# Softmax attention: moving three small PSUM users from the banks of P and V to the banks of the scores

## The chip, the core and the metric

The kernel runs on one NeuronCore of a Trainium2 chip. TensorE (PE in the profile; PEld is its weight load) multiplies and writes only to PSUM, VectorE (DVE) and ScalarE (ACT) read PSUM and work on it, GpSimd (POOL) works beside them, and SyncE (SP) issues most DMAs. Every engine takes its instructions in the order in which they were queued. The metric is the device time of one execution in microseconds (us); lower is better.

## The reference

The model is a trunk of two layers over 16 learned meta tokens and 1024 frames of width 1024 (T = 1040 positions). Each layer normalises, makes one wide projection, feeds it to two groups of attention heads, projects the concatenated result back and adds it, and then runs a gated feed-forward network. The change lies in the second head group, the softmax attention with a forget gate:

```python
logits = (jnp.einsum('bqhd,bkhd->bhqk', q_b, kf)
          + c_b[..., None] - c_k[:, :, None, :])
logits = jnp.where(key_pos[None, :] <= q_pos[:, None], logits, -jnp.inf)
return jnp.einsum('bhqk,bkhd->bqhd', jax.nn.softmax(logits, axis=-1), vf)
...
o_fox = rms_norm(o_fox, fox_norm[i].reshape(FOX_HEADS, FOX_DH))
```

There are 8 heads of width 64. The output of every head is normalised by its own root mean square and scaled before the output projection.

## The kernel before

Activations are kept transposed, with the 1024 features on 8 x 128 partitions and positions along the free axis. A float32 product is made of three float32r products of a high and a low part (`mm3`, lines 217 to 219: high by high, low by high, high by low), so most PE time stands on these lines. A layer runs through a gated linear attention (the `gla_` functions), the softmax attention (the `fox_` functions), the output projection, and the feed-forward network (`ffn_up`, `down_tiles`, `down_last`).

**The softmax stage.** `fox` (line 756) goes through 4 pairs of heads. The 1040 positions are cut into 9 query tiles, the first of 112 rows and the others of 116, which are taken in groups (7,8), (5,6), (3,4), (1,2), (0). A step is one query tile of one head: 72 steps per layer. In step `n`:

- `fox_scores` (line 638) makes the scores against all keys up to the tile's end, in up to three pieces: keys 0 to 459, 460 to 923 and 924 to 1039. Tiles 0 to 3 have one piece, tiles 4 to 7 two, tile 8 three, the third of them 116 keys short. Each piece takes one PSUM bank of the tag `S`: two matmuls (653, 654), then DVE adds the gate and keeps a running minimum of the negated scores (656), then, after the last piece's minimum, ACT takes the exponential with its row sum (668) and writes P to SBUF. With that the bank is free.
- `fox_transposes` (line 675) turns each piece of P by PE transposes into a PSUM bank of the tag `tr` (689; 682 for the short third piece, `ci == 2`), and ACT and DVE split it into a high and a low part in SBUF (331, 332). After DVE the bank is free.
- `fox_av` (line 692) multiplies P by V into a bank of the tag `av` (707), over all pieces of a group, and ACT copies the sum out (710). V carries its high and low part side by side, so that the sum's two halves must be added later.
- `fox_fold` (line 712) turns that result back by PE transposes (720) into a bank, the tile `fo`, where ACT (723) and DVE (724) add the two halves; then come the norm's small instructions.
- `fox_store` (line 739) transposes the normalised output again (746) into a bank, the tile `tr`, and ACT writes it with its scale (753) to SBUF for a DMA on POOL's queue (754). For the last pair it is split straight into the operand of the output projection (334, 335).

**What sets the order.** `fox_schedule` (line 827) sets delays: the transposes of step `n` are traced in step `n+2`, the products with V in `n+3` after the last tile of a group, fold in `n+4`, store in `n+6`. Between them, `work.run` traces matmuls of other work as filling: the projections of the next pair of heads (`fox_products`), a gate of the linear attention (`gr_products`), and at the end the output projection. `high_priority(8)` puts the scores a little ahead. This trace order is a priority only. Before the run, a planner with durations of its own decides the order on every engine: it takes the first instruction, by priority, whose inputs and whose buffer are free by its own clock. A tile's tag names the buffers it may take. On the chip this order is fixed, and semaphores hold an instruction whose input or buffer isn't free yet, and with it all that is queued behind it on its engine.

**The eight PSUM banks** of the stage are handed out in `attention` (line 866): two for `mm` (the filling's sums), three for `S`, two for `tr`, one for `av`. The transposes of V (587, in `fox_products`) take `tr` as well.

Of the kernel before, what the change touches and what calls it, by code (L numbers as in the profile page):

```python
# [10 lines left out]
F32 = mybir.dt.float32  # L11
# [122 lines left out]
class Kern:  # L134
# [540 lines left out]
    def fox_transposes(self, i, ci, P, PT, qoff, pp):  # L675
        nc = self.nc
        rows = self.rows_of(i)
        id_ = self.ident[:rows, :rows]
        tr = pp.tile([128, 4, 128], F32, tag="tr", name="tr")
        qs = slice(qoff, qoff + rows)  # L680
        if ci == 2:
            nc.tensor.transpose(tr[:FT, 0, :FT], P[:FT, :FT], id_)
            self.split(PT[2][:, 0, :], PT[2][:, 1, :], tr[:FT, 0, :FT])
            return
        nt = min(4 * ci + 4, i + 1) - 4 * ci
        for j in range(nt):
            t = 4 * ci + j
            o, w = self.start_of(t) - self.start_of(4 * ci), FT if i else FIRST
            nc.tensor.transpose(tr[:w, j, :rows], P[:rows, o:o + w], id_)  # L689
        self.split(PT[ci][:w, :nt, 0, qs], PT[ci][:w, :nt, 1, qs], tr[:w, :nt, :rows])  # L690
# [21 lines left out]
    def fox_fold(self, tiles, avs, den, ap, pp):  # L712
        nc = self.nc
        nt = len(tiles)
        rows = self.rows_of(tiles[0])
        fo = pp.tile([128, 2, 2, 2, 64], F32, tag="av", name="fo")
        for ti in range(nt):
            for e in range(2):
                w = rows
                nc.tensor.transpose(fo[:w, ti, e].rearrange("p a b -> p (a b)"),  # L720
                                    avs[:, e, FT * ti:FT * ti + w], self.ident[:])
        f = ap.tile([128, 2, 2, 64], F32, tag="ff", name="ff", bufs=1)
        nc.scalar.copy(f[:rows, :nt], fo[:rows, :nt, :, 0])
        nc.vector.tensor_tensor(out=f[:rows, :nt], in0=fo[:rows, :nt, :, 1], in1=f[:rows, :nt], op=ALU.add)
        on = sq = ap.tile([128, 2, 2, 64], F32, tag="fon", name="fon", bufs=1)
        nc.scalar.activation(sq[:rows, :nt], f[:rows, :nt], AF.Square)
        vv, d2, y0, a = (ap.tile([128, 2, 2], F32, tag=f"f{x}", name=f"f{x}", bufs=2)[:rows, :nt] for x in "vdya")
        nc.vector.scalar_tensor_tensor(out=d2, in0=den[:rows, :nt], scalar=64.0 * EPS,
                                       in1=den[:rows, :nt], op0=ALU.mult, op1=ALU.mult)
        nc.vector.tensor_reduce(out=vv, in_=sq[:rows, :nt], axis=AX.X, op=ALU.add)  # L730
        nc.vector.tensor_tensor(out=vv, in0=vv, in1=d2, op=ALU.add)
        fl = (lambda x: x) if nt == 2 else (lambda x: x[:, 0, :])
        self.rsqrt(fl(y0), fl(vv), fl(y0), fl(a), scale=1.0 / 64)
        for ti in range(nt):
            nc.vector.tensor_tensor(out=on[:rows, ti], in0=f[:rows, ti],
                                    in1=y0[:, ti, :].unsqueeze(2).to_broadcast([rows, 2, 64]), op=ALU.mult)
        return on

    def fox_store(self, lyr, p, tiles, on, ap, pp, mix):
        nc = self.nc  # L740
        n = FT * (len(tiles) - 1) + self.rows_of(tiles[-1])
        tr = pp.tile([128, 4, 128], F32, tag="tr", name="tr")
        trf = tr[:].rearrange("p a b -> p (a b)")
        for ti in range(len(tiles)):
            w = self.rows_of(tiles[ti])
            nc.tensor.transpose(trf[:, FT * ti:FT * ti + w],
                                on[:w, ti].rearrange("p a b -> p (a b)"), self.ident[:w, :w])
        c0 = self.start_of(tiles[0])
        if mix is not None:
            self.split(mix[0][:, c0:c0 + n], mix[1][:, c0:c0 + n], trf[:, :n], self.v(lyr, V_XN, p))  # L750
            return
        st = ap.tile([128, 2 * FT], F32, tag="fst", name="fst", bufs=1)
        nc.scalar.mul(st[:, :n], trf[:, :n], self.v(lyr, V_XN, p))
        nc.gpsimd.dma_start(self.mixd[4 + p][:, c0:c0 + n], st[:, :n])
# [689 lines left out]
```

## Time and profile before

| | |
|---|---|
| median of 3 runs | 2629.63 us (2625.71 to 2631.41) |
| the profiled execution's own time | 2631.03 us |
| its span, first to last instruction | 2629.3 us |
| mean granted TensorE clock | 0.989 |
| PE / PEld busy | 2526.3 us (96%) / 2407.3 us (92%) |
| DVE / ACT / POOL busy | 1751.8 us (67%) / 1241.9 us (47%) / 402.9 us (15%) |
| softmax stage of layer 0 / layer 1 | about 176 to 525 us / about 1480 to 1850 us |

How to read it: a row of waits tells which instruction an engine stood at and which instruction of another engine released it. For a tile's bank that means the reader who was last to leave the bank's earlier content. "PE tr L689 <- DVE PT L332" is a transpose that waited until DVE had finished with the bank. The views by time give the busy time of each engine in a stretch, and PEclk, the granted share of TensorE's full clock in it.

### The profile page before, as it was taken

To read this page: it belongs to the slowest core of one execution; us is meant where nothing else is said; L and a number is where in the kernel's file an instruction comes from. 1 tells how busy PE (TensorE), PEld (TensorE's weight loads), DVE (VectorE), ACT (ScalarE), POOL (GpSimd) and SP (SyncE) were. 2 spreads that over 40 slices of the span, in tenths; PEclk is the share of its full clock that TensorE was granted. 3 is DMA by queue.
4 is the path that set the end of the run, shared out by engine and by line. 5 is a ranking of instruction groups with operands and counts; after the bars stand their busy time and mean duration, and the time that the engine had idled before them with its cause. 6 is when DMAs were issued, how large, how long until landed. Compare 5 with 4: busy or idle time off the path is not lost.

```text
span 2629.3 us, 46309 instructions
## 1 busy us (share of the span) xinstructions
PE 2526.3 (96%) x18102; PEld 2407.3 (92%) x18102; DVE 1751.8 (67%) x3514; ACT 1241.9 (47%) x2677; POOL 402.9 (15%) x566
## 2 busy tenths in 40 slices
PE   8999999899999999999999999998999999999997
PEld 7988898898999999999999888888899999998886
DVE  7655766759877777643665665666698677776335
ACT  6345665635544445321443565665464444453112
POOL 4033333310000000000201333332100000000002
PEclk9999999999999999999999999999999999999999
DMA  3222123342322223522311222142523222245222
GB/s 124 67 83 71 44 86 122 105 145 89 105 77 83 80 81 100 209 90 59 106 52 66 75 73 74 56 133 92 164 73 113 79 79 74 84 154 179 62 57 75
DMA packets 117355, 245.96 MB, mean 94 GB/s; under 512 B 14752, under 2 KB 36512, under 8 KB 117136
## 3 DMA queue, kind: packets, MB, share of 16 engines
q1 hardware_dynamic: 97440, 184.89, 22.4%
q0 software_dynamic: 17824, 55.80, 6.2%
q8 instruction: 142, 2.33, 0.3%
q10 hardware_dynamic: 1872, 2.31, 0.2%
q14 instruction: 77, 0.63, 0.1%
HBM read 179.26 MB, written 50.91 MB: 88 GB/s over the span
## 4 chain that ended last, share of the span: by engine, by line
PE 76%; DVE 12%; issue 4%; ACT 4%; DMA 2%; POOL 1%; SPq 0%; DVEq 0%; POOLq 0%; ACTq 0%
PE mm L217 12%; PE mm L218 12%; PE mm L219 12%; PE up L217 9%; PE up L219 9%; PE up L218 9%; PE av L707 2%; PE tr L689 2%; DVE S L656 2%; PE wo L217 1%; PE wo L218 1%; PE wo L219 1%; DVE PT L332 1%; DVE x L1044 1%; DMA cb<-cd 1%
## 5 line engine op out<-in xcount | busy, mean ns | idle before, releaser
L217 PE MATMUL up<-x,hi 128*128 128x260 f32 (+1 forms) x2464 | 698.9, 284 | 2.3 <-ACT x L1043 1.6
L219 PE MATMUL up<-x,hi 128*128 128x260 f32 (+1 forms) x2464 | 697.8, 283 | 1.9 <-DVE x L1044 1.8
L218 PE MATMUL up<-x,lo 128*128 128x260 f32 (+1 forms) x2464 | 697.5, 283 | 0.8 <-DVE lo L1020 0.8
L219 PEld LDWEIGHTS up<-x,hi 128*128 128x128 f32 x2464 | 466.5, 189 | 2.9 <-DVE x L1044 2.9
L217 PEld LDWEIGHTS up<-x,hi 128*128 128x128 f32 x2464 | 465.9, 189 | 3.5 <-ACT x L1043 2.2
L218 PEld LDWEIGHTS up<-x,lo 128*128 128x128 f32 x2464 | 466.3, 189 | 1.0 <-DVE lo L1020 1.0
L217 PE MATMUL mm<-xh,hi 128*128 128x348 f32 (+4 forms) x1056 | 365.2, 346 | 0.0
L218 PE MATMUL mm<-xh,lo 128*128 128x348 f32 (+4 forms) x1056 | 340.9, 323 | 0.0
L219 PE MATMUL mm<-xl,hi 128*128 128x348 f32 (+4 forms) x1056 | 340.7, 323 | 0.0
L1020 DVE TENSOR_TENSOR lo<-raw,hi 128x512 fp32r<-128x512 f32 x308 | 210.1, 686 | 140.2 <-ACT hi L1019 140.2
L184 ACT CAST hi<-raw 128x512 fp32r<-128x512 f32 (+1 forms) x264 | 143.1, 544 | 334.0 <-PE mm L219 238.1
L218 PE MATMUL mm<-ah,lo 128*128 128x400 f32 (+1 forms) x760 | 266.5, 351 | 0.9 <-DVE lo L186 0.9
L219 PE MATMUL mm<-al,hi 128*128 128x400 f32 (+1 forms) x760 | 265.4, 349 | 0.0
L217 PE MATMUL mm<-ah,hi 128*128 128x400 f32 (+1 forms) x760 | 265.4, 349 | 0.0
L1019 ACT CAST hi<-raw 128x512 fp32r<-128x512 f32 x308 | 190.3, 621 | 113.8 <-PE up L219 87.2
L186 DVE TENSOR_TENSOR lo<-raw,hi 128x512 fp32r<-128x512 f32 (+1 forms) x196 | 110.8, 569 | 175.3 <-ACT hi L184 171.6
L217 PEld LDWEIGHTS mm<-xh,hi 128*128 128x128 f32 x1056 | 201.0, 190 | 6.0 <-issue 5.3
L218 PEld LDWEIGHTS mm<-xh,lo 128*128 128x128 f32 x1056 | 200.9, 190 | 0.4 <-issue 0.3
L219 PEld LDWEIGHTS mm<-xl,hi 128*128 128x128 f32 x1056 | 199.8, 189 | 0.4 <-issue 0.3
L668 ACT ACTIVATE P<-S,m 116x460 f32<-116x460 f32 (+2 forms) x224 | 125.1, 562 | 76.2 <-DVE m L656 72.1
L332 DVE TENSOR_TENSOR PT<-tr,PT 116x464 fp32r<-116x464 f32 (+3 forms) x240 | 122.1, 516 | 57.5 <-ACT PT L331 55.9
L218 PEld LDWEIGHTS mm<-ah,lo 128*128 128x128 f32 x760 | 142.8, 188 | 14.6 <-DVE lo L186 1.5
(248 smaller groups left out, 5106.5 us busy)
## 6 DMA issues: line engine op xcount, KB each, us to landing
raw<-in_wm_dram SPq DMA_DIRECT2D x338, 256.0 KB, 2.7
raw<-in_wd_dram SPq DMA_DIRECT2D x64, 256.0 KB, 2.7
actd<-cv POOLq DMA_DIRECT2D x22, 520.0 KB, 3.0
st<-actd SPq DMA_DIRECT2D x22, 520.0 KB, 4.6
actd<-cv POOLq DMA_DIRECT2D x22, 512.0 KB, 2.9
st<-actd SPq DMA_DIRECT2D x22, 512.0 KB, 4.9
cb<-cd SPq DMA_DIRECT2D x16, 520.0 KB, 4.2
kA<-kA SPq DMA_DIRECT2D x24, 260.0 KB, 3.8
```

The costliest lines, as they stand in the source:

```text
L184: nc.scalar.copy(hi[:, :n, :], raw[:, :n, :])
L186: eng.tensor_tensor(out=lo[:, :n, :], in0=raw[:, :n, :], in1=hi[:, :n, :].bitcast(F32), op=ALU.subtract)
L217: nc.tensor.matmul(ps, wh, xh[:, c0:c0 + n], start=first, stop=False, skip_group_check=more)
L218: nc.tensor.matmul(ps, wl, xh[:, c0:c0 + n], start=False, stop=False, skip_group_check=more)
L219: nc.tensor.matmul(ps, wh, xl[:, c0:c0 + n], start=False, stop=last, skip_group_check=more)
L332: nc.vector.tensor_tensor(out=lo, in0=src, in1=hi.bitcast(F32), op=ALU.subtract)
L656: nc.vector.tensor_tensor_reduce(out=S[:rows, :n], in0=S[:rows, :n], in1=cb[:rows, c0:k1], scale=1.0, scalar=(BIG if ci == 0 else m[:rows, ...
L668: nc.scalar.activation(P[:rows, :n], S[:rows, :n], AF.Exp, scale=-1.0, bias=m[:rows, nch - 1:nch], accum_out=(den if nch == 1 else d3[:row ...
L689: nc.tensor.transpose(tr[:w, j, :rows], P[:rows, o:o + w], id_)
L707: nc.tensor.matmul(av[:, a:width], w.rearrange("p a b -> p (a b)"), x, start=(t == 0 and i == 0), stop=(t == last and i == 1))
L1019: nc.scalar.copy(hi[:], src[:])
L1020: nc.vector.tensor_tensor(out=lo[:], in0=src[:], in1=hi[:].bitcast(F32), op=ALU.subtract)
```

## The change

Three tiles take a bank of another tag; nothing else is touched. The short third piece's transpose (8 per layer) and the output's transpose in `fox_store` (20 per layer) leave the two `tr` banks for the three `S` banks. The folded sums `fo` (20 per layer) leave the one `av` bank for the `S` banks. The numbers of banks per tag stay as they are.

```diff
@@ fox_transposes
-        tr = pp.tile([128, 4, 128], F32, tag="tr", name="tr")
+        tr = pp.tile([128, 4, 128], F32, tag="S" if ci == 2 else "tr", name="tr")
@@ fox_fold
-        fo = pp.tile([128, 2, 2, 2, 64], F32, tag="av", name="fo")
+        fo = pp.tile([128, 2, 2, 2, 64], F32, tag="S", name="fo")
@@ fox_store
-        tr = pp.tile([128, 4, 128], F32, tag="tr", name="tr")
+        tr = pp.tile([128, 4, 128], F32, tag="S", name="tr")
```

## The prediction

> **What bounds the kernel now.** I read the page first, then the busy times of the two softmax stages, then who waited for whom.
>
> ```profile
> span 2629.3 us, 46309 instructions
> PE 2526.3 (96%) x18102; PEld 2407.3 (92%) x18102; DVE 1751.8 (67%) x3514; ACT 1241.9 (47%) x2677; POOL 402.9 (15%) x566
> PE 76%; DVE 12%; issue 4%; ACT 4%; DMA 2%; POOL 1%; SPq 0%; DVEq 0%; POOLq 0%; ACTq 0%
> ```
>
> TensorE sets the time: 96% busy, and 76% of the chain that ended last. So the change is worth what it takes out of, or puts into, PE's idle time. The busy time by stretch (columns: stretch, its us, then busy us and instructions of PE, PEld, DVE, ACT, POOL, then PEclk, DMA share, GB/s):
>
> ```profile
> 176.00:525.00 349.00, 322.50 (x2221) 302.87 (x2219) 234.88 (x730) 212.85 (x636) 120.89 (x174) 0.99 0.28 85
> 1480.00:1850.00 370.00, 340.28 (x2316) 320.30 (x2315) 241.85 (x749) 216.98 (x649) 123.46 (x176) 0.98 0.28 84
> 476.00:496.00 20.00, 15.80 (x106) 14.28 (x105) 20.00 (x55) 16.67 (x47) 9.30 (x14) 0.91 0.46 145
> 1780.00:1800.00 20.00, 15.38 (x96) 13.71 (x95) 20.00 (x55) 15.60 (x45) 10.17 (x16) 0.83 0.51 159
> ```
>
> In the softmax stages PE is idle for 349 - 322.5 = 26.5 us and 370 - 340.3 = 29.7 us: 56 us that a better use of banks could touch. DVE is busy two thirds of the stage, but in one stretch of each layer, at the last pair of heads, all of it; waits there are DVE's own pace and no bank cures them. Who PE waited for (total us, times, longest):
>
> ```profile
> PE tr L689 <- DVE PT L332: 23.1, 22, 2.0
> PE tr L682 <- DVE PT L332: 12.1, 6, 3.4
> PE av L707 <- DVE ff L724: 8.8, 15, 1.0
> PE tr L746 <- DVE PT L332: 3.6, 8, 1.3
> PE tr L689 <- DVE ml L335: 1.0, 1, 1.0
> PE mm L218 <- POOL lo L186: 4.1, 6, 1.0
> PEld S L653 <- ACT P L668: 1.1, 4, 0.4
> ```
>
> The first five rows are all waits for a bank of `tr` or of `av`: 48.6 us of the 56. The scores, with three banks, waited 1.1 us in four places. That imbalance is what the change uses.
>
> **The work itself doesn't change.** All 16 short transposes, 144 fold transposes and 72 output transposes remain, with their readers on ACT and DVE and the store's DMA on POOL's queue; a bank of another tag makes none of them longer. What moves is who waits for which bank, and the planner's order with it.
>
> **Removed 1: the short piece, L682.** Here is one of its six waits, PE's rows first, then DVE's.
>
> ```profile
> 370.01 0.33 PE L707 MATMUL av<-PT,Vm 116*128 116x116 f32 x2
> 372.33 0.31 PE L682 MATMUL tr<-ident,Ps 116*116 116x116 f32 x1 [1.98 <-DVE PT L332]
> 372.40 0.40 PE L217 MATMUL mm<-xh,hi 128*128 128x344 f32 x1
> ...
> 368.67 0.34 DVE L616 TENSOR_SCALAR ge<-gx 128x348 f32<-128x348 f32 x1 [0.34 <-DMA mixd<-ge]
> 371.20 0.52 DVE L621 SCALAR_TENSOR_TENSOR ge<-ge,gy 128x348 f32<-128x348 f32 x1 [1.21 <-ACT gy L619]
> 371.63 0.63 DVE L332 TENSOR_TENSOR PT<-tr,PT 116x464 fp32r<-116x464 f32 x1
> ```
>
> The first two pieces hold both `tr` banks while ACT and DVE are late with them, behind a gate (L616 to L621) that waited for its DMA. The short piece, third in line, stands at the head of PE's queue, and filling that needs nothing (L217) stands behind it. With a bank of `S` it goes on as soon as one of three is free. I take 10 of the 12.1 us; what isn't got is where ACT, late as well, holds the scores' banks. Ends: 6 and 12.1.
>
> **Removed 2: the clock after these waits.** The granted clock behind three of the six:
>
> ```profile
> 373.10:376.60 3.50, 3.50 (x16) 3.32 (x15) 2.33 (x8) 0.79 (x2) 0.99 (x2) 0.51 0.31 102
> 1584.80:1588.30 3.50, 3.47 (x13) 3.30 (x14) 2.40 (x7) 0.76 (x3) 0.56 (x1) 0.51 0.32 102
> 1673.60:1680.50 6.90, 5.53 (x21) 5.35 (x22) 4.67 (x12) 3.49 (x11) 0.99 (x2) 0.51 0.16 52
> ```
>
> PE works at half clock for 3.5, 3.5 and 6.9 us right after. At 0.51, its 3.50 + 3.47 + 5.53 us of work there would take half: 6.1 us lost. Not every such gap does it, so other gaps may start to; I take 4 us, ends -6 (as much lost elsewhere) and 6.1. The Trainium skill, page "TensorE: Matmul & The Clock Gate", section "Why this matters for your kernels", warns only of idle gaps over about 3 us. The trace speaks against that: the gap of 1.98 us was enough. By the page's rule the longest wait alone (the 3.4) would count, the clock term would be 5.53 x 0.49 = 2.7 us, and the sum 1.3 us later.
>
> **Removed 3: `fo` in the bank of P and V, and the store in `tr`.** One wait of each, DVE's row that released the first above it, then the store and the transpose behind it, that one's last case, and the first and last of two transposes behind a short piece:
>
> ```profile
> 213.97 0.42 DVE L724 TENSOR_TENSOR ff<-fo,ff 116x256 f32<-116x256 f32 x1
> 214.44 1.16 PE L707 MATMUL av<-PT,V 112*128 112x232 f32 x8 [0.66 <-DVE ff L724]
> ...
> 221.57 0.42 PE L746 MATMUL tr<-ident,fon 116*128 116x116 f32 x2 [0.20 <-DVE PT L332]
> 222.68 0.41 PE L689 MATMUL tr<-ident,P 116*116 116x116 f32 x2 [0.69 <-DVE PT L332]
> ...
> 1797.05 0.64 PE L689 MATMUL tr<-ident,P 116*116 116x116 f32 x2 [0.29 <-DVE PT L332]
> ...
> 204.70 0.51 PE L689 MATMUL tr<-ident,P 116*116 116x116 f32 x3 [0.79 <-DVE PT L332]
> 1504.05 0.61 PE L689 MATMUL tr<-ident,P 116*116 116x116 f32 x4 [0.79 <-DVE PT L332]
> ```
>
> The wait behind `fo` is 8.8 us in all, the store's own 3.6. The L689 waits right behind a store are eight, from 0.69 to 0.29, together 5.3; those behind a short piece 2 x 0.79 = 1.6; L335, a store of the last pair, 1.0. That is 20.3 us. In or just after the two stretches where DVE is saturated lie 5.8 of them, which I give up: 14.5. Of these I take 60%, 8.7 us, because PE then comes sooner to the next L689, whose remaining waits (23.1 - 5.3 - 1.6 = 16.2 us) are for eviction by the same ACT and DVE. Ends: 0 and 14.5.
>
> **Added: users of the `S` banks.** Durations of what works in a bank (count, total us, mean ns):
>
> ```profile
> L653 PE MATMUL S<-kA,qA 128*116 128x460 f32 (+4 forms) x240 | 88.0, 367 | 0.1
> L654 PE MATMUL S<-kL,qA 128*116 128x460 f32 (+4 forms) x240 | 83.8, 352 | 0.0
> L656 DVE CUSTOM_DVE_ANT_0 S<-S,cb 116x460 f32<-116x460 f32 (+2 forms) x144 | 80.6, 560 | 58.8 <-PE S L654 58.4
> L668 ACT ACTIVATE P<-S,m 116x460 f32<-116x460 f32 (+2 forms) x224 | 125.1, 562 | 76.2 <-DVE m L656 72.1 <-DVE fv L731 2.3
> L720 PE MATMUL fo<-ident,avs 128*116 128x128 f32 x144 | 22.3, 273 | 0.0
> L723 ACT COPY ff<-fo 116x256 f32<-116x256 f32 (+1 forms) x40 | 14.1, 354 | 16.1 <-PE fo L720 15.4
> L724 DVE TENSOR_TENSOR ff<-fo,ff 116x256 f32<-116x256 f32 (+1 forms) x40 | 15.7, 393 | 5.3 <-ACT ff L723 4.5
> L753 ACT ACTIVATE fst<-tr,vec 128x232 f32<-128x232 f32 (+1 forms) x30 | 13.0, 434 | 13.2 <-PE tr L746 13.2
> ```
>
> A score piece works 0.37 + 0.35 + 0.56 + 0.56 = 1.84 us in its bank, 240 of them 442 us. The 40 `fo` bring about 0.56 + 0.35 + 0.39 = 1.3 us each, the 40 stores 0.42 + 0.43 = 0.85, the 16 short pieces about as much: 100 us, a fifth more on three banks. No row shows these three waiting for an `S` bank, or a score behind them; if they do, PE holds its filling behind it, ACT its exponentials, and POOL, at the store's DMA, the splits L186 that PE already waited 4.1 us for. Two bounds, per allocation: the scores' own 1.1 / 240 = 0.005 us, and the two `tr` banks' (23.1 + 12.1 + 3.6 + 1.0) / 304 = 0.13 us (240 pieces, 40 stores, 24 of V). For 240 + 96 = 336 allocations that is 2 to 44 us. The one `av` bank lies between, 8.8 / 120 = 0.07. Three banks with a fifth more load are nearest to their own row: I take 0.02, 7 us.
>
> **The sum**, from the profiled execution's own 2631.0: -10 - 4 - 8.7 + 7 = -15.7, so 2615.3. The median is 1.4 us under that execution and both lie within the runs' spread, so I forecast 2615.
>
> **The rivals.**
> *The scores' banks become the bound (slower).* Place: the start of each of the 8 head pairs, tiles 8 and 7, where the steps want 3, 2, 3 and 2 banks and two short pieces, a fold and two stores of the pair before fall in. For it: waits behind one late gate (1.98 us above) hold scores and newcomers alike. Against it: 1.1 us of waits so far. At 0.10 us per allocation, 34 us, it gives 2631 - 25 + 34 = 2640, with the relief left whole without a clock gain (10 + 14.5); it decides from 25 / 336 = 0.074 us on.
> *The waits come again at the next transpose.* The planner issues by its own clock; given free banks it packs transposes tighter, and PE stands at L689 for the same late DVE. For it: 16.2 us of L689 waits have no store or short piece in front. Then only the `av` waits outside the saturated stretches go (6.8 us) and `S` costs 4: 2628, no change.
> *More than forecast.* All of 12.1 + 14.5, the whole clock term 6.1, and `S` at its own rate (2): 2631 - 31 = 2600; with the likely losses 2603.
> *The change does nothing* because a short piece really waits for its data is excluded: its releaser is L332 of an earlier piece, not its exponential.
>
> **How the numbers follow.** Forecast 0.50 (2605 to 2624), more 0.10, waits again 0.21, scores' banks 0.19. The range 2601 to 2640 leaves out part of the second and about half of the last. From no change a measurement of this kernel tells about 0.2%, 5 us: faster is the first two and a little of the third, 0.61; same 0.20; slower 0.19.
>
> **What would show it.** Right: no row L682 <- PT L332 and no L707 <- ff L724 among PE's waits, L746 gone, L689 under 19 us, L653 or L720 waiting some 7 us for L668 or L724, and full clock where the short pieces are. Wrong: waits of `S` (L653, L682, L720, L746) summing to over 25 us, PE idle in the softmax stages no less than 56 us, or stages no shorter though the waits are gone.

## The result and the profile after

The changed kernel takes 2617.1 us (median of five runs, 2614.6 to 2620.0) against 2627.8 us: a ratio of 0.995, 95% interval 0.9939 to 0.9961, so 0.5% faster. The forecast was 2615 in a range of 2601 to 2640. The total was met; two of its terms were not, as the parts will show. A few executions of the kernel before and of two others took 3.5 to 10.9 ms and are left out of every time and ratio here; one of them is the only profiled execution of the kernel with the short piece and the store, so no profile of that kernel is read.

The page after:

```profile
span 2615.7 us, 46303 instructions
PE 2522.8 (96%) x18102; PEld 2411.3 (92%) x18102; DVE 1751.2 (67%) x3514; ACT 1237.7 (47%) x2677; POOL 403.2 (15%) x566
```

PE, DVE, ACT and POOL carry out as many instructions as before. To see where the 13.6 us of span went, each softmax stage is cut at its first score and at the first matmul of the output projection outside it. Busy time of the engines in these two stretches, before:

```profile
180.00:550.50 370.50, 341.70 (x2333) 321.39 (x2331) 242.78 (x754) 218.25 (x651) 124.22 (x177) 0.99 0.28 86
1479.40:1853.20 373.80, 343.45 (x2333) 323.07 (x2331) 243.00 (x754) 218.38 (x651) 124.43 (x177) 0.98 0.28 85
sum 744.30, PE 685.15 PEld 644.46 DVE 485.78 ACT 436.62 POOL 248.65; mean PE 342.58 PEld 322.23 DVE 242.89 ACT 218.31 POOL 124.33
```

and after:

```profile
179.70:544.10 364.40, 340.03 (x2334) 322.99 (x2331) 242.31 (x754) 217.15 (x651) 124.51 (x177) 0.99 0.29 87
1473.70:1837.70 364.00, 339.37 (x2333) 322.61 (x2331) 242.03 (x754) 217.06 (x651) 124.89 (x177) 0.99 0.29 88
sum 728.40, PE 679.40 PEld 645.61 DVE 484.33 ACT 434.21 POOL 249.40; mean PE 339.70 PEld 322.80 DVE 242.17 ACT 217.10 POOL 124.70
```

The two stages lost 744.3 - 728.4 = 15.9 us; the rest of the kernel gave 2.3 back. PE's idle time there, length less busy time, fell from 59.2 to 49.0 us, by 10.2. Its busy time fell by 5.8 us for the same matmuls, part of it because fewer of them ran at half clock (27.3 us of the stages before, 20.5 after, by the trace's record of the granted clock). Who PE waited for, after:

```profile
PE tr L689 <- DVE PT L332: 15.7, 14, 2.2
PE S L653 <- ACT P L668: 11.2, 10, 1.8
...
PE mm L217 <- ACT hi L184: 5.8, 4, 2.7
PE mm L218 <- POOL lo L186: 5.6, 8, 1.0
...
PE av L707 <- DVE PT L332: 2.8, 7, 0.7
```

The waits of the short piece for DVE (12.1 us before), of P and V for the fold (8.8), of the store (3.6) and of L335 (1.0) have no row any more, and the transposes wait 15.7 us instead of 23.1. In their place the scores wait 11.2 us for a bank. And one row is quite new: filling that waits 5.8 us for the high part of a weight (L184), which the prediction had not named.

The new waits at the scores sit where the short piece stood before. PE after, and ACT beside it:

```profile
281.58 0.33 PE L707 MATMUL av<-PT,Vm 116*128 116x116 f32 x2
281.75 0.29 PE L682 MATMUL tr<-ident,Ps 116*116 116x116 f32 x1
...
283.90 0.47 PE L653 MATMUL S<-kA,qA 128*116 128x460 f32 x1 [1.23 <-ACT P L668]
```

```profile
281.67 0.59 ACT L618 ACTIVATE gy<-ge,ones 128x348 f32<-128x348 f32 x1
282.29 0.49 ACT L619 ACTIVATE gy<-gy 128x348 f32<-128x348 f32 x1
282.69 0.53 ACT L331 CAST PT<-tr 116x464 fp32r<-116x464 f32 x1
283.11 0.65 ACT L668 ACTIVATE P<-S,m 116x460 f32<-116x460 f32 x1
```

The short piece goes through without a wait, 0.9 us of filling follow, and then the next score stands until ACT, late behind the same gate (L618, L619), has done the exponential that holds a bank. There are six such places, from 1.22 to 1.78 us, 8.2 us together; before, the short piece stood there for 12.1 us in six waits.

### The profile page after: what moved, and what is told of

The parts are those of the page before. It is cut to its first block, busy times and chain, and to the rows that moved or that the text cites. A ratio compares the mean times of both kernels' runs of the same rounds, so it can differ in the third digit from the quotient of the medians.

```text
span 2615.7 us, 46303 instructions
## 1 busy us (share of the span) xinstructions
PE 2522.8 (96%) x18102; PEld 2411.3 (92%) x18102; DVE 1751.2 (67%) x3514; ACT 1237.7 (47%) x2677; POOL 403.2 (15%) x566
## 4 chain that ended last, share of the span: by engine, by line
PE 62%; issue 17%; DVE 13%; ACT 4%; DMA 2%; POOL 2%; SPq 0%; DVEq 0%; POOLq 0%; ACTq 0%
PE mm L217 12%; PE mm L218 12%; PE mm L219 12%; PE up L219 5%; PE up L217 5%; PE up L218 5%; PE av L707 2%; DVE S L656 2%; PE tr L689 2%; PE wo L217 1%; PE wo L218 1%; PE wo L219 1%; ACT P L668 1%; DVE x L1044 1%; DVE PT L332 1%
## 5 line engine op out<-in xcount | busy, mean ns | idle before, releaser
L217 PE MATMUL up<-x,hi 128*128 128x260 f32 (+1 forms) x2464 | 698.8, 284 | 2.0 <-ACT x L1043 1.4
L217 PEld LDWEIGHTS up<-x,hi 128*128 128x128 f32 x2464 | 465.8, 189 | 3.1 <-ACT x L1043 2.0
L217 PE MATMUL mm<-xh,hi 128*128 128x348 f32 (+4 forms) x1056 | 363.6, 344 | 0.0
L184 ACT CAST hi<-raw 128x512 fp32r<-128x512 f32 (+1 forms) x264 | 143.0, 544 | 330.0 <-PE mm L219 239.1
L217 PE MATMUL mm<-ah,hi 128*128 128x400 f32 (+1 forms) x760 | 265.4, 349 | 0.0
L217 PEld LDWEIGHTS mm<-xh,hi 128*128 128x128 f32 x1056 | 199.6, 189 | 5.9 <-issue 5.3
L668 ACT ACTIVATE P<-S,m 116x460 f32<-116x460 f32 (+2 forms) x224 | 124.8, 561 | 103.5 <-DVE m L656 101.2
```

The costliest lines, as they stand in the source:

```text
L184: nc.scalar.copy(hi[:, :n, :], raw[:, :n, :])
L217: nc.tensor.matmul(ps, wh, xh[:, c0:c0 + n], start=first, stop=False, skip_group_check=more)
L668: nc.scalar.activation(P[:rows, :n], S[:rows, :n], AF.Exp, scale=-1.0, bias=m[:rows, nch - 1:nch], accum_out=(den if nch == 1 else d3[:row ...
```

## The experiments

Each part of the change was run alone, in pairs and all together; then the two suspects, the fold at the last pair and the gate, were varied. Ratios are to the kernel before, run on the same chip as the kernel in question; "stages" is the length of both softmax stages and "idle" PE's idle time in them, from the profile of one execution. Each kernel has an order of its own, made anew by the planner; no run kept the order and changed a bank alone.

| in the scores' banks | ratio, 95% interval | stages us | idle us |
|---|---|---|---|
| nothing (before) | 1 | 744.3 | 59.2 |
| short piece | 0.9988, 0.9979 to 0.9996 | 739.9 | 59.3 |
| fold | 1.0033, 1.0021 to 1.0046 | 751.4 | 63.3 |
| store | 0.9971, 0.9962 to 0.9981 | 735.8 | 54.0 |
| fold, store | 0.9981, 0.9968 to 0.9994 | 738.6 | 54.5 |
| short piece, fold | 1.0002, 0.9991 to 1.0012 | 743.3 | 60.2 |
| short piece, store | 0.994, 0.9927 to 0.9953 | | |
| all three (after) | 0.995, 0.9939 to 0.9961 | 728.4 | 49.0 |

### The short piece alone

```diff
@@ fox_transposes
-        tr = pp.tile([128, 4, 128], F32, tag="tr", name="tr")
+        tr = pp.tile([128, 4, 128], F32, tag="S" if ci == 2 else "tr", name="tr")
```

> Only the short third piece's transpose takes a bank of the scores; the fold and the store stay where they were. Theory A (each tile is worth its own waits): the 12.1 us of L682 go, but the profile after shows the scores (L653) waiting about 1.2 us for the exponential behind each of the same six late gates, 8.2 us in all, so some 4 us of waits are left as gain and 2 to 4 us of clock: 2620 to 2623 against 2628, with L653 <- L668 at 7 to 9 us. Theory B (DVE and ACT set the pace, the waits come again at the next transpose): L689 <- L332 grows by what L682 loses, no change, 2625 to 2630. Theory C (a new order by the planner, unrelated to the waits): any time between 2615 and 2640, and waits that don't match it.

Measured: 2625.9 us, ratio 0.9988. Its waits of PE:

```profile
PE tr L689 <- DVE PT L332: 28.7, 31, 2.1
PE av L707 <- DVE ff L724: 9.5, 16, 1.2
...
PE tr L746 <- DVE PT L332: 4.9, 8, 1.2
PE S L653 <- ACT P L668: 4.7, 7, 1.3
```

L682 is gone, but L689 has 5.6 us more, the scores 4.7, the store 1.3 and P and V 0.7: together 12.3, as much as the 12.1 that L682 gave. The two stages:

```profile
sum 739.90, PE 680.64 PEld 639.32 DVE 485.37 ACT 435.96 POOL 248.55; mean PE 340.32 PEld 319.66 DVE 242.68 ACT 217.98 POOL 124.28
```

Idle time 739.9 - 680.6 = 59.3 us, as before; busy time 4.5 us less. So B was right about the idle time, and the small gain is in PE's busy time. By the trace's record of the granted clock, half clock in the stages fell from 27.3 to 17.1 us, and half of that difference is 5.1 us.

### The fold alone

```diff
@@ fox_fold
-        fo = pp.tile([128, 2, 2, 2, 64], F32, tag="av", name="fo")
+        fo = pp.tile([128, 2, 2, 2, 64], F32, tag="S", name="fo")
```

> Only the folded sums leave the bank of P and V for the scores' banks. Theory A: the 8.8 us of L707 <- L724 go, 2 to 3 us come back as L707 <- L332, 1 to 2 us of waits of the scores are added, L682 keeps its 12 us: 2621 to 2624 against 2628. Theory B: L689 and L682 take the time over, 2626 to 2630. Theory C: any time between 2615 and 2640.

Measured: 2638.0 us, ratio 1.0033: slower, which neither A nor B had; theory C's range holds it, but says nothing of why. Its waits:

```profile
PE tr L689 <- DVE PT L332: 21.2, 24, 2.2
PE tr L682 <- DVE PT L332: 16.8, 6, 4.0
...
PE tr L746 <- DVE PT L332: 5.9, 8, 1.6
PE mm L217 <- ACT hi L184: 5.9, 4, 2.7
```

P and V no longer wait for the fold, 8.8 us less, but the short piece waits 4.7 us more, the store 2.3, and the filling 5.9 us for a weight. The scores have 0.2 us of waits: their banks were not the price. In the stages PE's idle time is 4.1 us longer than before, and half clock rose from 27.3 to 41.0 us.

### The store alone

```diff
@@ fox_store
-        tr = pp.tile([128, 4, 128], F32, tag="tr", name="tr")
+        tr = pp.tile([128, 4, 128], F32, tag="S", name="tr")
```

> Only the output's transpose in the store leaves the two banks of the transposes for the scores' banks. Theory A: L746's 3.6 us, L335's 1.0 and the eight L689 waits behind a store, 5.3 us, go, less what lies in the stretch where DVE is saturated; 1 to 2 us of waits of the scores are added: 2620 to 2624 against 2628, L689 <- L332 from 23 to about 18 us. Theory B: L689 stays at 23 us, 2626 to 2630. Theory C: any time between 2615 and 2640.

Measured: 2620.6 us, ratio 0.9971, as A had it. L746 is gone, L689 falls to 19.8 us (about 18 were expected), L682 stays at 12.6, idle time falls by 5.2 us. The store is the part that pays most by itself.

### Two of the three

> The fold and the store take the scores' banks, the short piece stays with the transposes: the change without its part for L682. Theory A: the gains of the two add, 2616 to 2620, and what the full change gains over this (to 2617) is small, 0 to 4 us, because the scores wait at the same late gates in the short piece's place. Theory B: no more than 3 us under 2628. Were the short piece the main part, as the prediction had it (10 us and 4 us of clock against 8.7 us for fold and store), this would be 2621 to 2624.

Measured, fold and store: 2622.2 us, ratio 0.9981. So the full change gains 0.3% over it, some 8 us, more than the 0 to 4 that A allowed. The time lies above A's bounds and within those that were named for the short piece as the main part: beside the other two, its move does pay. PE's idle time in the stages falls by 54.5 - 49.0 = 5.5 us with it, where alone it saved none.

> The short piece and the fold take the scores' banks, the store stays with the transposes. Theory D: the fold's harm alone came through L682 (16.8 us) and L746 (5.9 us) standing at the transposes' banks; with the short piece moved as well, L682 is gone, L653 <- L668 takes about 8 us, L217 <- L184 stays near 6: 2624 to 2630. If the parts simply added (-3 and +9): 2635.

Measured, short piece and fold: 2631.5 us, ratio 1.0002. The waits are theory D's: no L682, L653 12.3 us, L217 <- L184 5.8 us; the time is a little above its bounds.

> The short piece and the store take the scores' banks, the fold stays in the bank of P and V. So far: short piece alone 2626, store alone 2621, fold alone 2638, fold and store 2622, all three 2617, none 2628 to 2629. Theory D (idle time of TensorE plus half of the time at half clock accounts for the differences; the fold alone lost by a wait for a weight's high part, L217 <- L184, 5.9 us, longer waits of L682 and more time at half clock): this one has no L217 <- L184 wait and no L682 wait, keeps about 9 us of L707 <- L724, and ends at 2615 to 2620, as good as all three. Theory C (a lottery of the planner's order): not told apart from 2610 to 2630 by the sum of parts.

Measured, short piece and store: 2613.7 us (2610.4 to 2615.5), ratio 0.994, just under theory D's bounds; what D said of its waits can't be looked up without a profile. It is as fast as all three: within the intervals, moving the fold as well brings nothing.

From the table, a part is worth what it changes beside each set of the others. The store: -0.3, -0.5, -0.5 and -0.5%. The short piece: -0.1, -0.3, -0.3 and -0.3%. The fold: +0.3, +0.1, +0.1 and +0.1%. Each of these differences is uncertain by somewhat under 0.2%, so a single one of 0.1% proves nothing; but no sign changes.

### Where the fold does its harm

The new wait for a weight lies in the last pair of heads of each layer. PE after, and ACT before it:

```profile
495.84 0.29 PE L689 MATMUL tr<-ident,P 116*116 116x116 f32 x1
498.85 0.39 PE L217 MATMUL mm<-mh,hi 128*128 128x256 f32 x1 [2.73 <-ACT hi L184]
```

```profile
493.15 0.37 ACT L723 COPY ff<-fo 116x256 f32<-116x256 f32 x1 [0.64 <-PE fo L720]
494.02 0.42 ACT L726 ACTIVATE fon<-ff 116x256 f32<-116x256 f32 x1 [0.49 <-DVE ff L724]
495.12 0.20 ACT L272 ACTIVATE fy<-fv 116x4 f32<-116x4 f32 x1 [0.69 <-DVE fv L731]
495.36 0.20 ACT L273 ACTIVATE fy<-fy 116x4 f32<-116x4 f32 x1
497.20 0.55 ACT L668 ACTIVATE P<-S,m 116x344 f32<-116x344 f32 x1 [1.64 <-DVE m L656]
...
498.17 1.15 ACT L184 CAST hi<-raw 128x512 fp32r<-128x512 f32 x2
```

The cast of the weight (L184) stands in ACT's queue behind the fold's norm, which goes back and forth between ACT and DVE, and behind an exponential that waits for DVE. PE stands 2.73 us, and then works at half clock for 6.8 us (the second row is the same place in the other layer):

```profile
499.50:506.50 7.00, 6.30 (x28) 6.30 (x29) 1.81 (x5) 1.20 (x5) 2.29 (x3) 0.51 0.21 75
1793.20:1800.10 6.90, 6.11 (x28) 6.11 (x29) 1.82 (x6) 1.29 (x5) 2.39 (x3) 0.51 0.26 80
```

Two kernels tell whether it is the fold at this place. The first is the changed kernel with the last pair's fold back in its old bank (`fox_fold` takes the tag as an argument for this):

```diff
-            st["on"] = self.fox_fold(tiles, st["avs"], st["den"], ap, pp)
+            st["on"] = self.fox_fold(tiles, st["avs"], st["den"], ap, pp, "av" if p == 3 else "S")
```

> The changed kernel, but for the last pair of heads of each layer the folded sums stay in the bank of P and V. Theory D: the two waits of 2.7 us for a weight's high part (L217 <- L184) and the 6.8 us of half clock right behind each came with the fold's move at the last pair; they go, about 1 us of L707 <- L724 comes back twice: 2608 to 2614 against 2617. If they come from the order as a whole, they stay or move, and the time is 2614 to 2620.

Measured: 2605.0 us, ratio 0.9906 (0.9892 to 0.9921), below the interval of the full change and 3 us below theory D's bounds. It is also below the interval of the short piece and the store (0.9927 to 0.9953): for the first three pairs the fold's move pays, about 0.3%. The profiled execution took 2612.6 us, the longest of the five (the others 2602.9 to 2607.9), so its profile shows less than the whole gain. Its waits and its stages:

```profile
PE tr L689 <- DVE PT L332: 19.6, 20, 2.0
PE S L653 <- ACT P L668: 11.4, 10, 1.8
...
PE mm L218 <- POOL lo L186: 4.1, 6, 1.0
...
PE av L707 <- DVE ff L724: 2.9, 2, 1.9
```

```profile
sum 722.60, PE 676.57 PEld 643.63 DVE 485.45 ACT 434.65 POOL 248.64; mean PE 338.29 PEld 321.81 DVE 242.73 ACT 217.33 POOL 124.32
```

No L184 is left among the waits. PE's idle time in the stages is 46.0 us against 49.0 in the full change, half clock 17.1 against 20.5 us. The cast starts no earlier here (498.53 us), but it stands ahead of the fold's L726 in ACT's queue, and PE still has filling of the weight before, up to 499.8 us. So the fold's move changed the order on both engines.

The second is its complement, `"S" if p == 3 else "av"`.

> The complement of fold_by_pair: short piece and store in the scores' banks, and the fold there for the last pair of heads alone, with P and V for the first three pairs. Theory D (the fold's harm sits at the last pair): the waits L217 <- L184 of 5.8 us come back, most of L707 <- L724 of the first pairs stays, and the time is 2620 to 2627, 5 to 12 us over the kernel without the fold's move (2614, ratio 0.994). If the harm doesn't sit there, it is within 4 us of that.

Measured: 2623.7 us, ratio 0.9971 (0.996 to 0.9981), slower than without any move of the fold (0.994). L217 <- L184 is back at 5.9 us. In the profiles that could be read, this wait stands in every kernel that has the last pair's fold in the scores' banks, and in none that hasn't. That the harm comes with the fold at this place is thereby shown; how much of it is this wait with the half clock behind it, and how much the rest of the new order, was not measured apart.

### The gate

The changed kernel, with the gate's last product written over its loaded operand, which has two buffers, in place of the exponential's single one:

```diff
-            to = e if dst is None else dst[:, c0:c0 + n]
+            to = og if dst is None else dst[:, c0:c0 + n]
...
-                nc.gpsimd.dma_start(self.mixd[h][:, c0:c0 + n], e)
+                nc.gpsimd.dma_start(self.mixd[h][:, c0:c0 + n], og)
```

> The changed kernel, and the gate writes its product over its loaded operand (two buffers) instead of over its exponential's one buffer, so that the next gate doesn't wait for the DMA of the last one. Theory A': the gate in front of the six waits of the scores (8.2 us) is late by its own chain between DVE and ACT more than by the DMA: 1 to 3 us less, 2613 to 2617. If the DMA is what makes it late, L653 <- L668 falls below 5 us and the time to 2608 to 2612.

Measured: 2612.7 us, ratio 0.9935 (0.9922 to 0.9947); L653 <- L668 9.0 us. Its interval overlaps that of the full change, so its gain by itself is not shown; the scores' waits shrink a little, not below 5: the DMA is the smaller part of the gate's delay. In the changed kernel the gate's first instruction (L616) had waited 0.7 us for it in two places, here in none.

Then the gate's sigmoid was left out of both kernels:

```diff
-            nc.vector.tensor_scalar(out=e, in0=x, scalar1=-87.0, scalar2=None, op0=ALU.max)
-            nc.scalar.activation(e, e, AF.Exp, scale=-1.0)
-            nc.scalar.activation(y, e, AF.Ln, bias=self.ones[:, 0:1])
-            nc.scalar.activation(y, y, AF.Exp, scale=-1.0)
...
+            nc.vector.tensor_tensor(out=to, in0=x, in1=og, op=ALU.mult)
```

> The kernel before with the gate's sigmoid left out (the maximum, three functions of ACT and three instructions of DVE per gate unit; what remains is two products). Theory A'': the late chain of the gate is what the short piece waited for: L682 <- L332 falls from 12.1 us to under 3; 10 to 20 us faster than the kernel before. Rival: the two banks are too few by themselves: L682 keeps 8 us or more.

Measured: 2606.4 us, ratio 0.9906 (0.9893 to 0.992), 25 us less where 10 to 20 were expected. PE's wait at the short piece's transpose (L674 in this kernel) is 0.3 us in all. So the gate made those 12 us, and for the short piece the two banks were enough without it. (Leaving it out takes work from DVE and ACT everywhere in the stage and gives the planner a new order; its lateness at these places is not set apart from that.)

> The changed kernel with the gate's sigmoid left out in the same way. Theory A'': L653 <- L668 falls from 11.2 us to under 5, and the change is worth 4 to 9 us against the same kernel without it. Rival: the scores' banks are too few by themselves: L653 keeps 8 us or more, and the change is worth its 11 us or none.

Measured: 2597.3 us, ratio 0.9871 (0.9858 to 0.9885). Waits (L645, L660 are the scores and the exponential here):

```profile
PE tr L681 <- DVE PT L332: 15.9, 16, 1.4
...
PE mm L217 <- ACT hi L184: 5.9, 4, 2.7
...
PE S L645 <- ACT P L660: 3.0, 4, 1.3
```

The scores' waits fall from 11.2 to 3.0 us: they too were the gate's. The change is worth 2606.4 - 2597.3 = 9.1 us without the sigmoid, uncertain by about 5 us, with the two intervals apart. So at least a good part of its gain doesn't hang on the gate, and most of it by the medians.

### Both improvements together

> fold_by_pair and gate_og together. If the two gains add (12 and 4 us under the changed kernel): 2600 to 2603, ratio 0.988 to 0.990. If the planner's order undoes one: 2604 to 2612.

Measured: 2602.2 us (2600.1 to 2603.0), ratio 0.9887 (0.9872 to 0.9902): 1.1% under the kernel before, as in the first expectation, and the lowest time of all kernels with the full computation. Its interval overlaps that of the fold by pair alone (0.9892 to 0.9921), so what the gate adds is not shown here either. Its stages take 720.8 us, PE is idle for 44.2 us of them.

## Why the prediction was right

**The bound.** Right: TensorE's idle time in the two stages was the thing to look at. 10.2 us of idle time and 5.8 of busy time went there, and the rest of the kernel gave 2.3 back.

**Removed 1, the short piece (10 us).** Too high. The row L682 went, as foretold, but the step counted as got what the next instruction then waited for. Alone, the move changed idle time by nothing (59.2 to 59.3 us), and the largest part of the wait came again at L689: the second rival's mechanism. Beside the fold and the store it saved 5.5 us of idle time, just under the step's lower end of 6; there, 8.2 us of waits stand at the scores behind the same gate. The step spoke of ACT, late as well, holding the scores' banks, and priced it at 2 us. What the DVE and ACT behind the gate had not finished, no bank could replace.

**Removed 2, the clock (4 us).** Right in the places named: the stretches behind the three short pieces, 13.7 us at half clock before, are at full clock in the trace after. But at the last pair half clock rose from 10.2 to 20.5 us, and four windows of 3.4 us of that stand right behind the new waits for a weight. In the stages it fell from 27.3 to 20.5 us, worth half of the difference, 3.4 us, which is near the 4. Over the whole execution it did not fall: the mean granted clock is 0.989 in both profiled executions, because there is as much more half clock outside the stages, for example at 31.9 us, long before the first of them. The step's lower end had named this case (as much lost elsewhere). So the term was met in the stages alone, and no run shows it as a gain of the whole.

**Removed 3, the fold and the store (8.7 us).** The store's part held: alone it gives 0.3%, L746 and L335 have no row after, and L689 ended at 15.7 us, under the 19 that was set as the mark. The fold's part had the wrong sign when moved for all pairs. Its 8.8 us of waits did vanish, but the move made new ones, above all at the last pair. The step took an instruction's own wait for the worth of its removal, less a share, and for the fold it did not ask what the planner would put earlier with it.

**Added, the scores' banks (7 us).** 11.2 us at L653: above the value taken, 0.033 instead of 0.02 us per allocation, and well inside the bounds 2 to 44. The slower rival needed 0.074 and did not come. The mere number of users was not the price either: with fold and store there, 80 of the 96 new users, the scores waited 0.2 us and the fold 1.6 us. It was mostly the gate that made three banks scarce: without its sigmoid the scores waited 3.0 us.

**The sum.** -15.7 us were forecast for one execution; its span fell by 13.6, and the runs' medians by 10.7. That it came so near is in part luck: the short piece gave less than its term, the store more beside the others than alone, the fold took some back, and the clock's gain in the stages was lost outside them. The direction and the bound were right; the sum was right by balance, not in each term.

## What to carry to other kernels

A wait for a buffer names the last reader of that buffer, and that reader may itself be late for a reason elsewhere: here a gate's chain across two engines. Another buffer then moves the wait to the next instruction that needs the same late engines; take the suspect away, as with the sigmoid, before counting the wait as a gain. Where a planner makes the order, try each part of a change alone and at each place: the fold's move paid for three pairs of heads and cost at the fourth.

## What the runs showed of the hardware

The length of a gap alone did not decide whether the clock fell. In the changed kernel PE stood for 2.19 us at a transpose. The view by stretch of time shows the 3.41 us before the drop, and half clock right behind it:

```profile
478.91 0.71 PE L689 MATMUL tr<-ident,P 116*116 116x116 f32 x3 [2.19 <-DVE PT L332]
...
475.68:479.09 3.41, 1.22 (x10) 0.89 (x9) 3.41 (x10) 3.26 (x10) 2.05 (x2) 1.00 0.22 52
...
479.10:482.50 3.40, 3.37 (x15) 2.92 (x13) 3.40 (x9) 2.29 (x6) 1.62 (x3) 0.50 0.39 117
```

The longest waits at the scores, up to 1.8 us, show no drop after them. The Trainium skill, page "TensorE: Matmul & The Clock Gate", section "Why this matters for your kernels", sets its warning at about 3 us. These traces don't bear out such a length: in the kernel before, a gap of 1.85 us was followed by half clock at 444.68 us and another of 1.85 us at 285.09 us was not; in the kernel with the fold alone, a gap of 3.28 us was not:

```profile
288.25 0.31 PE L682 MATMUL tr<-ident,Ps 116*116 116x116 f32 x1 [3.28 <-DVE PT L332]
...
282.97:286.38 3.41, 2.01 (x17) 1.87 (x15) 1.79 (x10) 1.30 (x4) 0.00 (x0) 1.00 0.31 87
286.38:289.80 3.42, 1.54 (x9) 1.33 (x9) 3.24 (x10) 3.13 (x10) 0.95 (x2) 1.00 0.00 0
```

What fits all of them is how much PE worked in one step of the record. In each of the 13 profiles that were read, the granted clock changes only at whole steps of 3.41 us, and the stretches above are cut at these steps. The 2.19 us lie within one step, with 1.22 us of work in it; the 3.28 us are shared by two, with 2.01 and 1.54 us. In these profiles, without the first 40 and the last 12 us of each, every step at full clock in which PE was busy for less than 45% was followed by half clock, 70 of 70; between 45 and 60% it was 33 of 110; above that 6 of 9382, none of them in a softmax stage. This is a count over traces, not a test of its own. It agrees with the reading that a few short gaps cost less than one long one of the same sum: with the short piece moved alone, PE's idle time stayed, half clock fell from 27.3 to 17.1 us, and 4.5 us of PE's busy time went.
